# Seven half-size products instead of eight in the gated feed-forward layers of a diffusion trunk

## The chip, the cores and the metric

The kernel runs on one core of a Trainium2 chip. Its engines work side by side, each through its own queue in order: TensorE (PE in the profile) multiplies matrices into PSUM, VectorE (DVE) and ScalarE (ACT) work elementwise and read PSUM, GpSimd (POOL) works elementwise on SBUF, and SyncE (SP) issues the loads from DRAM. The metric is the device time of one execution in microseconds, lower is better.

## The reference

A trunk of two layers runs over 512 latent and 256 context tokens of 1024 channels. Each layer has a gated feed-forward half-step, a token mixer (a diagonal state space model "S5" in the first layer, gated linear attention "GLA" in the second) and a second feed-forward half-step; every one of these is preceded by an RMS norm whose scale, shift and gate come from a conditioning vector (adaLN). Cut to the part that matters here:

```python
def rmsnorm(x, w):
    return x * lax.rsqrt(jnp.mean(x * x, axis=-1, keepdims=True) + NORM_EPS) * w

def swiglu_ffn(h, w_in, w_out):                 # w_in (1024, 2 * 2816), w_out (2816, 1024)
    g, u = jnp.split(jnp.einsum('bld,df->blf', h, w_in), 2, axis=-1)
    return jnp.einsum('blf,fd->bld', jax.nn.silu(g) * u, w_out)

def ffn_half_step(x, w_norm, shift, scale, gate, w_in, w_out):
    h = rmsnorm(x, w_norm) * (1.0 + scale) + shift
    return x + 0.5 * gate * swiglu_ffn(h, w_in, w_out)

mod_x = jnp.einsum('bd,de->be', jax.nn.silu(c), ada_w[i]) + ada_b[i]    # adaLN: 9 * 1024 columns
```

All data are float32. There are four feed-forward half-steps; this document counts them one to four. Steps one, two and three are computed for all 768 tokens, step four for the latent tokens only.

## The kernel before

**Layout.** The residual stream `xT` lies in SBUF with channels on the 128 partitions: 8 channel tiles of 768 tokens. A float32 product is made of float32r parts: each operand is split into `hi` (rounded by ScalarE) and `lo` (the remainder, made by VectorE), and `mm3` (L109 to L115) adds three matmuls, hi x hi, hi x lo and lo x hi. The normed tokens are `h`, both parts, 8 channel tiles.

**Weights.** `weight` (L77) loads a unit of 128 x 1024 from DRAM into one of four buffers `wraw`, ScalarE casts it to `whi` (L88) and VectorE makes `wlo` (L89). `slot` (L92) gives the place: five pairs, or eight while the pool `more` is open, which it is during steps two and three.

**A feed-forward step** (`ffn`, L221). The hidden layer has 22 tiles of 128 columns, each with a gate and a value half. `unit(j)` (L247) loads both halves of tile j, one unit each. `hidden` (L251) multiplies the 8 channel tiles of each half by a range of tokens into two PSUM banks, then silu on ScalarE (L263), the product on VectorE (L264), and the split of the result into `mh` (L265) and `ml` (L266). Most tiles go over two ranges of 384 tokens (`parts`); the first four tiles (`lead`) go over thirds of 256 tokens (`first`), so that the norms of later tokens run while the first third is multiplied. After each group of hidden tiles (`bounds`: 4, 4, 4, 2, 4, 4) `product` (L268) multiplies them with `w_out` and adds the gated sum to `xT` on VectorE (L275). The last group goes by thirds of the tokens (`last`), and each finished third starts the norm of the next step (`after`).

**Norms.** `squares` (L142) sums squares over channel tiles on ScalarE and VectorE. The rest is put off by a counted number of steps (`later`, `tick`, L118 to L122): the sums over partitions and Newton's steps for 1/sqrt (`rstd`, L154), three steps later `spread` (L178) brings the result to all partitions, and `rest` (L196) scales each channel tile (L201) and splits it into `h` with the shift (`split`, L215: ScalarE L218, VectorE L219). `ensure` (L128) issues at once whatever is still put off that the tokens to come need.

**Fillers.** The adaLN modulation of later norms is computed beside the hidden tiles: `by_vector` (L426) loads one block of 1024 x 512 weights as four units into `wraw`, multiplies and adds them on VectorE (L435, L437: 16 operations of 512 columns), transposes and sums (L442, L443), and ends with four small matmuls. `fill` gives a list of such blocks, six in step two and nine in step three, and `filler` (L240) issues them evenly between the tiles.

**Order.** The program is written in an order of priority; a scheduler that simulates the engines' times fixes each engine's queue from it when the kernel is built. In between steps one and two stands the S5 mixer, which ends in a gated product (`glu`, L923) whose last three of eight output tiles go by thirds, as they start the norms of step two.

Of the kernel before, what the change touches and what calls it, by code (L numbers as in the profile page):

```python
# [8 lines left out]
F32 = mybir.dt.float32  # L9
F32R = mybir.dt.float32r  # L10
# [14 lines left out]
UNIT = 1024        # columns of a unit of weights  # L25


def fview(t, off, dims, p0=0, n=P):
    """A view of a tile: partitions p0..p0+n, the free dims as (step, count) pairs from element off."""
    b = t[p0:p0 + n]  # L30
    return bass.AP(b.tensor, b.offset + off, [list(b.ap[0])] + [list(d) for d in dims])


def dview(ap, off, dims):
    """A view of a DRAM tensor with dims as (step, count) pairs from element off of the AP."""
    return bass.AP(ap.tensor, ap.offset + off, [list(d) for d in dims])


class Core:
    """Shared pools, constants and the building blocks used by every phase."""  # L40

    def __init__(self, tc, stack):
# [18 lines left out]
        self.more, self.nmore = None, 0  # L61

# [29 lines left out]
    def slot(self, hi, dtype=F32R):  # L92
        """A unit's place: one of five, or of those of a further pool."""
# [6 lines left out]

    def raw(self):
# [7 lines left out]
    def mm3(self, out, w, wcols, a, first, last):  # L109
        """out += w^T a with w = (hi, lo), a = (hi, lo) pairs of f32r APs."""  # L110
# [17 lines left out]
    def ensure(self, token=TOK):  # L128
        """No work is put off any more that tokens before this one need."""
# [48 lines left out]
    def spread(self, y):  # L178
        """Columns of 128 tokens to [P, tokens] in PSUM, the same on every partition."""
# [29 lines left out]
    def norm_split(self, s, e, sc, sh, steps=0, gap=3):  # L209
        """The norm into the operand h."""  # L210
# [3 lines left out]

    def split(self, hi, lo, t, col):  # L215
        """(hi, lo) = t + col, exactly in two f32r parts."""
# [4 lines left out]
    def ffn(self, tokens, first, parts, last, gate, w_in, w_out, mids_pool, fill=lambda: (), after=None, early=0,  # L221
            spared=0, ending=None):
# [1391 lines left out]
```

## Time and profile before

| | |
|---|---|
| median of three runs | 2954.92 us (2949.38 to 2956.03) |
| span of the profiled execution | 2955.6 us |
| instructions | 45053 |
| mean granted TensorE clock | 0.971 |
| POOL instructions | 40, all short |
| loads of `w_in`, `w_out`, `ada_w` into `wraw` | 176, 88 and 97 of 512 KB |

The profiled execution's span lies inside the three runs. The page gives each engine's busy time over the span and then follows the chain of work that ended last, back from the last instruction. Busy shares are means over stages: the span cut in forty slices shows where they differ.

```profile
PE   6999999997899999999999999999999899899997
DVE  8798988635686365646435665666368777643434
PEclk9999999998899999999999999999999899899998
```

Each digit is the busy share of a slice of 74 us in tenths. Steps two and three are slices 15 to 30, where PE's row is all nines and DVE's is mostly 3 to 6; step one is slices 2 to 10, with the preparation of the S5 mixer on VectorE beside it.

### The profile page before, as it was taken

To read this page: it belongs to the slowest core of one execution; us is meant where nothing else is said; L and a number is where in the kernel's file an instruction comes from. 1 tells how busy PE (TensorE), PEld (TensorE's weight loads), DVE (VectorE), ACT (ScalarE), POOL (GpSimd) and SP (SyncE) were. 2 spreads that over 40 slices of the span, in tenths; PEclk is the share of its full clock that TensorE was granted. 3 is DMA by queue.
4 is the path that set the end of the run, shared out by engine and by line. 5 is a ranking of instruction groups with operands and counts; after the bars stand their busy time and mean duration, and the time that the engine had idled before them with its cause. 6 is when DMAs were issued, how large, how long until landed. Compare 5 with 4: busy or idle time off the path is not lost.

```text
span 2955.6 us, 45053 instructions
## 1 busy us (share of the span) xinstructions
PE 2835.5 (96%) x18303; PEld 2640.2 (89%) x18303; DVE 1813.1 (61%) x4006; ACT 891.4 (30%) x1432; POOL 8.7 (0%) x40
## 2 busy tenths in 40 slices
PE   6999999997899999999999999999999899899997
PEld 4999999997558999999999999999998788788886
DVE  8798988635686365646435665666368777643434
ACT  6321121223645242121213321111245453332221
POOL 0000000000000000000000000000000000000000
PEclk9999999998899999999999999999999899899998
DMA  7434444524776123423311342434202112233320
GB/s 227 129 101 127 106 126 125 145 90 142 229 241 181 43 65 108 121 72 107 93 58 58 93 122 86 124 98 114 56 20 86 44 51 65 65 116 98 93 79 29
DMA packets 396045, 305.45 MB, mean 103 GB/s; under 512 B 57994, under 2 KB 344188, under 8 KB 395836
## 3 DMA queue, kind: packets, MB, share of 16 engines
q1 hardware_dynamic: 382908, 289.97, 33.5%
q10 hardware_dynamic: 12928, 12.59, 1.3%
q8 instruction: 144, 2.36, 0.3%
q14 instruction: 65, 0.53, 0.1%
HBM read 275.77 MB, written 30.41 MB: 104 GB/s over the span
## 4 chain that ended last, share of the span: by engine, by line
PE 84%; DVE 9%; DMA 3%; ACT 3%; issue 2%; SPq 0%; ACTq 0%; DVEq 0%
PE bank L113 24%; PE bank L114 24%; PE bank L115 24%; PE bank L412 2%; DVE s5e L514 1%; DVE s5g L514 1%; DVE wlo L89 1%; PE bank L818 1%; PE aux L715 1%; PE aux L1244 1%; DVE s5t L514 1%; PE bank L182 1%; PE bank L1112 1%; PE bank L1113 1%; PE bank L1111 1%
## 5 line engine op out<-in xcount | busy, mean ns | idle before, releaser
L114 PE MATMUL bank<-h,whi 128*128 128x384 f32 (+3 forms) x3160 | 1052.7, 334 | 1.8 <-DVE h L939 1.8
L115 PE MATMUL bank<-h,wlo 128*128 128x384 f32 (+3 forms) x3160 | 1052.2, 334 | 0.0
L113 PE MATMUL bank<-h,whi 128*128 128x384 f32 (+3 forms) x3160 | 1048.0, 335 | 3.2 <-ACT whi L88 1.8
L88 ACT CAST whi<-wraw 128x1024 fp32r<-128x1024 f32 (+1 forms) x321 | 335.8, 1048 | 983.8 <-PE bank L114 948.3
L114 PEld LDWEIGHTS bank<-h,whi 128*128 128x128 f32 (+1 forms) x3160 | 599.2, 190 | 19.9 <-DVE h L939 2.5
L113 PEld LDWEIGHTS bank<-h,whi 128*128 128x128 f32 (+1 forms) x3160 | 596.3, 190 | 22.7 <-ACT whi L88 2.1
L115 PEld LDWEIGHTS bank<-h,wlo 128*128 128x128 f32 (+1 forms) x3160 | 597.9, 189 | 17.0 <-issue 0.2
L89 DVE TENSOR_TENSOR wlo<-wraw,whi 128x1024 fp32r<-128x1024 f32 (+1 forms) x321 | 390.7, 1219 | 282.9 <-ACT whi L88 274.0
L114 PE MATMUL bank<-ml,whi 128*128 128x384 f32 (+2 forms) x1360 | 444.6, 328 | 0.0
L115 PE MATMUL bank<-mh,wlo 128*128 128x384 f32 (+2 forms) x1360 | 444.0, 328 | 0.0
L113 PE MATMUL bank<-mh,whi 128*128 128x384 f32 (+2 forms) x1360 | 443.3, 330 | 0.2
L264 DVE TENSOR_TENSOR sg<-sg,bank 128x384 f32<-128x384 f32 (+2 forms) x166 | 89.7, 540 | 382.5 <-PE bank L115 370.6
L275 DVE SCALAR_TENSOR_TENSOR xT<-bank,hg,xT 128x256 f32<-128x256 f32 (+3 forms) x488 | 229.2, 500 | 132.3 <-PE bank L115 131.4
L113 PEld LDWEIGHTS bank<-mh,whi 128*128 128x128 f32 x1360 | 255.8, 188 | 7.8 <-ACT mh L265 0.8
L115 PEld LDWEIGHTS bank<-mh,wlo 128*128 128x128 f32 x1360 | 255.9, 188 | 6.6 <-issue 0.2
L114 PEld LDWEIGHTS bank<-ml,whi 128*128 128x128 f32 x1360 | 256.0, 188 | 6.5 <-issue 0.2
L437 DVE SCALAR_TENSOR_TENSOR adaacc<-wraw,cs,adaacc 128x512 f32<-128x512 f32 x266 | 187.6, 746 | 22.5 <-DMA wraw<-in_ada_w_dram 22.2
L265 ACT CAST mh<-sg 128x384 fp32r<-128x384 f32 (+2 forms) x166 | 83.4, 503 | 384.3 <-DVE sg L264 383.7
L263 ACT ACTIVATE sg<-bank 128x384 f32<-128x384 f32 (+2 forms) x166 | 79.4, 478 | 181.9 <-PE bank L115 181.3
L266 DVE TENSOR_TENSOR ml<-sg,mh 128x384 fp32r<-128x384 f32 (+2 forms) x166 | 89.8, 541 | 32.1 <-ACT mh L265 31.9
L150 ACT ACTIVATE sq<-xT 128x256 f32<-128x256 f32 (+1 forms) x126 | 52.9, 428 | 77.2 <-DVE xT L275 54.5
L151 DVE TENSOR_TENSOR ssq<-ssq,sq 128x256 f32<-128x256 f32 (+1 forms) x126 | 54.8, 436 | 28.6 <-ACT sq L150 26.7
(306 smaller groups left out, 2557.7 us busy)
## 6 DMA issues: line engine op xcount, KB each, us to landing
wraw<-in_ffn_w_in_dram SPq DMA_DIRECT2D x176, 512.0 KB, 4.0
wraw<-in_ada_w_dram SPq DMA_DIRECT2D x97, 512.0 KB, 3.7
wraw<-in_ffn_w_out_dram SPq DMA_DIRECT2D x88, 512.0 KB, 3.5
wraw<-in_gla_w_in_dram SPq DMA_DIRECT2D x24, 512.0 KB, 3.9
s5R<-s5r ACTq DMA_DIRECT2D x16, 512.0 KB, 3.6
s5O<-s5g SPq DMA_DIRECT2D x64, 128.0 KB, 2.4
wlo<-in_ada_w_dram SPq DMA_DIRECT2D x16, 512.0 KB, 8.1
wraw<-in_s_w_glu_dram SPq DMA_DIRECT2D x16, 512.0 KB, 4.0
```

The costliest lines, as they stand in the source:

```text
L88: nc.scalar.copy(out=hi[:, :n], in_=raw[:, :n])
L89: nc.vector.tensor_tensor(out=lo[:, :n], in0=raw[:, :n], in1=hi[:, :n].bitcast(F32), op=ALU.subtract)
L113: mm(out, wh, a[0], start=first, stop=False)
L114: mm(out, wh, a[1], start=False, stop=False)
L115: mm(out, wl, a[0], start=False, stop=last)
L263: nc.scalar.activation(sg, banks[0][:, :e - s], AF.Silu)
L264: nc.vector.tensor_mul(sg, sg, banks[1][:, :e - s])
L265: nc.scalar.copy(out=mh[:, o], in_=sg)
L266: nc.vector.tensor_tensor(out=ml[:, o], in0=sg, in1=mh[:, o].bitcast(F32), op=ALU.subtract)
L275: nc.vector.scalar_tensor_tensor(out=self.xT[:, d, a:z], in0=b[:, a - s:z - s], scalar=gate[i][:, d:d + 1], in1=self.xT[:, d, a:z], op0=AL ...
L437: nc.vector.scalar_tensor_tensor(out=acc[:, v], in0=w[:, k], scalar=col, in1=acc[:, v], op0=ALU.mult, op1=ALU.add)
L514: self.c.nc.vector.tensor_tensor(out=out, in0=a, in1=b, op=op)
```

## The change

In steps two and three the first product of a hidden tile is done by Strassen's method in Winograd's form. The 8 channel tiles are cut in an upper and a lower half, the tokens in blocks of 128 that are even or odd, and a tile's columns in gate and value. That makes a product of 2 x 2 blocks by 2 x 2 blocks, which takes seven block products in place of eight, each over 4 channel tiles and half of the tokens.

- `unit` loads the same two units as before. GpSimd makes four sums of half-units in place, and `half` splits each of seven half-units of 512 columns into its two parts, two half-units to a slot.
- `norm_seven` replaces the split of the norm: beside the four blocks of `h` it makes four further sums on VectorE, three of which go with both parts into a new tile `hx`; it uses four `wraw` buffers for each 256 tokens.
- `hidden_seven` runs the seven products, each into a bank of its own (84 matmuls over half of the tokens), and VectorE combines them: seven sums that each read a bank, two products, two remainders.
- One leading tile in place of four, over the token ranges (0, 512) and (512, 768); the other 21 tiles go over all tokens at once.
- adaLN blocks are given to the filler in quarters (one load and four VectorE operations each, the finish with the last).
- The pool `more` isn't open in these steps (the slots are five pairs); in `glu` the last two tiles go by thirds, not three.

The core of the diff (comments that fall away, and the renaming of arguments, are left out):

```diff
+    def half(self, raw):
+        nc = self.nc
+        if self.pending is None:
+            self.pending = w = self.slot(True), self.slot(False)
+            hi, lo = (t[:, :HALF] for t in w)
+        else:
+            hi, lo = (t[:, HALF:] for t in self.pending)
+            self.pending = None
+        nc.scalar.copy(out=hi, in_=raw)
+        nc.vector.tensor_tensor(out=lo, in0=raw, in1=hi.bitcast(F32), op=ALU.subtract)
+        return hi, lo
...
+    def norm_seven(self, s, e, sc, sh, steps=0, gap=3):
...
+        def rest(y):
+            r = self.spread(y)
+            for g in range(2):
+                v, w = (self.raw().rearrange("p (a i t) -> p a i t", i=2, t=t) for t in (2 * P, P))
+                for i in range(2):
+                    for lower in range(2):
+                        k, t = 4 * lower + 2 * g + i, v[:, lower, i]
+                        nc.vector.scalar_tensor_tensor(out=t, in0=self.xT[:, k, s:e], scalar=sc[:, k:k + 1], in1=r,
+                                                       op0=ALU.mult, op1=ALU.mult)
+                        nc.scalar.activation(t, t, AF.Identity, bias=sh[:, k:k + 1])
...
+                for x, minuend, less, (hi, lo) in ((b11, None, None, place(0, 0)), (t1, b12, b11, place(0, 1)),
+                                                   (t2, b22, t1, beside(0)), (b21, None, None, place(1, 0)),
+                                                   (t3, b22, b12, beside(1)), (b22, None, None, place(1, 1)),
+                                                   (t4, b21, t2, beside(2))):
+                    if less is not None:
+                        nc.vector.tensor_tensor(out=x, in0=minuend, in1=less, op=ALU.subtract)
+                    nc.scalar.copy(out=hi, in_=x)
+                    nc.vector.tensor_tensor(out=lo, in0=x, in1=hi.bitcast(F32), op=ALU.subtract)
...
-        lead = 4 if self.more else 2
-        bounds = [0, 4, 8, 12, 14, 18, FT] if self.more else [0, 2, 6, 10, 14, 18, FT]
+        lead = 1 if seven else 4 if self.more else 2
+        bounds = [0, 4, 8, 12, 14, 18, FT] if self.more or seven else [0, 2, 6, 10, 14, 18, FT]
...
+            def both(out, i0, i1, op):
+                nc.gpsimd.tensor_tensor(out=out, in0=i0, in1=i1, op=op)
+                return self.half(out)
+            return [self.half(a11), both(a21, a21, a22, ALU.add), both(a11, a21, a11, ALU.subtract), self.half(a12),
+                    both(a21, a22, a11, ALU.subtract), both(a12, a12, a11, ALU.subtract), self.half(a22)]
+
+        def hidden_seven(j, w, s, e):
...
+            nc.scalar.copy(out=g1, in_=part(0, 0))
+            p5 = part(1, 1)
+            plus(g2, g1, part(2, 4))
+            plus(g1, g1, part(3, 2))
+            nc.scalar.activation(g1, g1, AF.Silu)
+            plus(u1, g2, part(4, 5))
+            plus(g2, g2, p5)
+            plus(u2, u1, p5)
+            plus(g2, g2, part(5, 3))
+            nc.scalar.activation(g2, g2, AF.Silu)
+            nc.vector.tensor_mul(u2, u2, g2)
+            mid(u2, 1)
+            plus(u1, u1, part(6, 6))
+            nc.vector.tensor_mul(u1, u1, g1)
+            mid(u1, 0)
...
-            if j < KT - 3:
+            if j < KT - 2:
...
+        return [lambda p=p: unit(p) for p in range(3)] + [lambda: (unit(3), finish())]
...
-                ffn(0, 1, both, thirds, halves, thirds, mp,
-                    lambda: rest(6, mp) + [lambda: (mods.scale(1, 0), mods.half_gate(1, 0))], norm(1, 0))
+                ffn(0, 1, both, pieces, halves, thirds, mp,
+                    lambda: rest(6, mp) + [lambda: (mods.scale(1, 0), mods.half_gate(1, 0))], norm_seven(1, 0),
+                    seven=True)
```

More of the change, by code (lines that the diff above doesn't have):

```diff
@@ L25 @@
 UNIT = 1024
+HALF = UNIT // 2
 def fview(t, off, dims, p0=0, n=P):
@@ L248, in unit @@
             mids[j] = [mids_pool.tile([P, n], F32R, tag=t, name=t, bufs=nfc) for t in ("mh", "ml")]
-            return [self.weight(win[:, :, q * F + j * P:q * F + (j + 1) * P]) for q in range(2)]
+            if not seven:
+                return [self.weight(win[:, :, q * F + j * P:q * F + (j + 1) * P]) for q in range(2)]
+            raw = [self.raw() for q in range(2)]
+            for q in range(2):
+                self.dma(raw[q].rearrange("p (k f) -> p k f", k=KT), win[:, :, q * F + j * P:q * F + (j + 1) * P])
@@ L283, in ffn @@
             for j in range(lead):
-                hidden(j, ws[j], s, e, j == 0)
+                if seven:
+                    hidden_seven(j, ws[j], s, e)
+                else:
+                    hidden(j, ws[j], s, e, j == 0)
         todo = list(fill())
@@ L291, in ffn @@
                 w = unit(j)
-                for s, e in parts:
-                    hidden(j, w, s, e, False)
+                if seven:
+                    hidden_seven(j, w, *tokens)
+                else:
+                    for s, e in parts:
+                        hidden(j, w, s, e, False)
                 filler()
@@ L438, in by_vector, with finish @@
                                                        op0=ALU.mult, op1=ALU.add)
[L439 to L450 removed]
+        def finish():
+            sums = pool.tile([P, 32], F32, tag="adas", name="adas", bufs=1)
+            for v in range(2):
+                turned = self.c.tmp.tile([P, 512], F32, tag="sg", name="adat", bufs=2)
+                nc.vector.transpose(turned, acc[:, v])
+                nc.vector.tensor_reduce(out=sums[:, 16 * v:16 * v + 16], in_=turned.rearrange("p (b x) -> p b x", x=32),
+                                        axis=mybir.AxisListType.X, op=ALU.add)
+            t = self.c.aux()
+            for g in range(4):
+                nc.tensor.matmul(t[32 * g:32 * g + 32, :8], self.quarter, fview(sums, g, [(4, 4), (16, 2)]),
+                                 start=True, stop=True)
+            self.columns(l, m, q, t)
+        return [lambda p=p: unit(p) for p in range(3)] + [lambda: (unit(3), finish())]
     def columns(self, l, m, q, t):
```

95 lines of the change are left out of this document (69 added, 26 removed).

## The prediction

> **What bounds the kernel now.** I read the profile's page first: engine totals, then the chain of work that ended last.
>
> ```profile
> PE 2835.5 (96%) x18303; PEld 2640.2 (89%) x18303; DVE 1813.1 (61%) x4006; ACT 891.4 (30%) x1432; POOL 8.7 (0%) x40
> PE 84%; DVE 9%; DMA 3%; ACT 3%; issue 2%; SPq 0%; ACTq 0%; DVEq 0%
> ```
>
> TensorE (PE) is on the path for 84% of the span, and POOL does nearly nothing. A mean says little of one stage, so I cut the span into windows. Feed-forward step two runs from about 1046 to 1605 us and step three to about 2173 (the bursts of xT updates by L275 show the ends).
>
> ```profile
> 1046.00:1605.00 559.00, 559.00 (x3502) 557.11 (x3501) 290.22 (x518) 130.00 (x208) 0.00 (x0) 1.00 0.29 85
> 1605.00:2173.00 568.00, 565.11 (x3556) 562.42 (x3555) 329.81 (x604) 130.09 (x209) 0.37 (x3) 1.00 0.32 94
> 1750.00:1800.00 50.00, 50.00 (x292) 49.73 (x292) 31.95 (x53) 10.01 (x14) 0.00 (x0) 1.00 0.39 112
> 1050.00:1100.00 50.00, 50.00 (x424) 50.00 (x423) 25.34 (x68) 18.82 (x41) 0.00 (x0) 1.00 0.01 3
> ```
>
> The columns after each window's length are the busy time and count of PE, weight loads, DVE (VectorE), ACT (ScalarE) and POOL, then the granted clock, DMA share and GB/s. PE never rests in step two and only 3 us in step three, at a clock of 1.00; DVE is busy 52% and 58%. **Both steps are bound by the number of matmuls.** The last two rows give the price: 50/292 = 0.171 us for a matmul with 384 columns, 50/424 = 0.118 us with 256.
>
> **What TensorE saves.** A hidden tile now takes 96 matmuls of 384 columns (2 halves, 2 products, 8 channel tiles, 3 terms): 16.4 us. After, 7 products x 4 x 3 = 84 of 384: 14.4 us, 2.05 less. Four tiles of each step go by thirds now, 144 x 0.118 = 17.0 us each; three of them come to 14.4, the first to 84 of 256 and 84 of 128 columns. No 128-column matmul of this kind is in the trace. Following the line from 384 to 256 gives 0.065 us; the bounds are that and 0.118, which would add 4.5 us a step. I take 0.065, so the first tile costs 15.4. Per step: 18 x 2.05 + 3 x 2.6 + 1.6 = 46.3; two steps **-93 us**. The gated product ahead of them moves one tile from thirds to halves: 17.0 - 16.4, -0.5. The last products of the steps stay.
>
> **What VectorE gets.** Durations in both steps, by shape:
>
> ```profile
> L89 DVE TENSOR_TENSOR wlo<-wraw,whi 128x1024 fp32r<-128x1024 f32 x128 | 156.4, 1222 | 116.4 <-ACT whi L88 115.6
> L437 DVE SCALAR_TENSOR_TENSOR adaacc<-wraw,cs,adaacc 128x512 f32<-128x512 f32 x210 | 147.8, 745 | 16.0 <-DMA wraw<-in_ada_w_dram 15.6
> L266 DVE TENSOR_TENSOR ml<-sg,mh 128x384 fp32r<-128x384 f32 x72 | 39.6, 551 | 16.2 <-ACT mh L265 16.2
> L264 DVE TENSOR_TENSOR sg<-sg,bank 128x384 f32<-128x384 f32 x72 | 39.5, 549 | 217.8 <-PE bank L115 215.3 <-PE aux L448 2.5
> L442 DVE STREAM_TRANSPOSE adat<-adaacc 128x512 f32<-128x512 f32 x30 | 21.1, 703 | 0.1
> L443 DVE TENSOR_REDUCE adas<-adat 128x16 f32<-128x512 f32 x30 | 20.3, 676 | 0.2
> L514 DVE TENSOR_TENSOR s5t<-s5asc,s5ct x32: 669/681/768, 186.1 to 558.8; 128x512 f32<-128x512 f32 x32
> ...
> 2140.69 0.55 DVE L266 TENSOR_TENSOR ml<-sg,mh 128x384 fp32r<-128x384 f32 x1
> 2141.16 0.48 DVE L275 SCALAR_TENSOR_TENSOR xT<-bank,hg,xT 128x256 f32<-128x256 f32 x1
> ```
>
> The last two rows, from the timeline, show that in a full queue the next instruction starts 0.08 us before the end of the one in front: a 384-column operation occupies 0.47 us, not 0.55. I subtract 0.08 throughout. A tile now takes 2 weight splits of 1024 columns and 4 operations of 384: 2 x 1.14 + 4 x 0.47 = 4.2 us. After, it takes 7 splits of 512 (0.681, so 0.60) and 11 operations of 384 (seven sums that each read a PSUM bank, two products and two remainders): 7 x 0.60 + 11 x 0.47 = 9.4 us. That is +5.2 a tile, +114 a step. Against the windows: 290 + 114 + 16 (norms, below) = 420 of 513 us in step two, 330 + 130 = 460 of 519 in step three. Can PE stay full beside that?
>
> ```profile
> 150.00:200.00 50.00, 50.00 (x316) 49.68 (x316) 45.26 (x139) 13.75 (x22) 0.52 (x1) 1.00 0.37 110
> ```
>
> Yes: in step one DVE is 91% busy in this window and PE does not rest. But it is closer inside the tiles. A quarter block of adaLN is 4 x 0.70 plus a quarter of the finish (two transposes, two sums, 0.7): 3.5 us. 24 quarters over 26 filler steps make 3.2 us a tile in step two, 36 make 4.85 in step three. So DVE has 12.6 us of work beside 14.4 of PE in step two, and **14.25 beside 14.4 in step three**; there nothing is left to hide a wait in.
>
> **What POOL gets.** Four sums of 128x512 a tile. The trace has no such operation; the nearest rows:
>
> ```profile
> L514 DVE TENSOR_TENSOR s5g<-s5asc,s5ct x32: 1097/1133/1220, 196.1 to 554.9; 128x512 f32<-128x512 f32 x32
> L670 POOL MEMSET s5cb<- 128x512 f32 x8 | 4.2, 525 | 504.1 <-PE aux L715 484.2 <-PE bank L1441 19.9
> masks.py:199 POOL TENSOR_SCALAR_AFFINE_SELECT ident<-ident 128x128 f32<-128x128 f32 x1 | 0.3, 292 | 0.0
> masks.py:197 POOL MEMSET ident<- 128x128 f32 x1 | 0.2, 204 | 0.3 <-POOLq L1603 0.3
> 336.05 4.12 DVE L514 TENSOR_TENSOR s5g<-s5asc,s5ct 128x512 f32<-128x512 f32 x4 [0.87 <-PE aux L715]
> ```
>
> The memsets give 0.10 us plus 0.84 ns a column, the one that reads a tile 1.5 ns a column; with a second input 2.2, so 1.23 us for 512 columns, an estimate. The bounds are 0.525 (only writing) and 1.66 (twice the one that reads). Four are 4.9 us of 14.4, so POOL itself is no bound; a half is ready about 2.5 us after its sum starts (sum, ACT's copy, DVE's split), and the five weight slots hold ten halves of which a tile uses seven, so that chain is hidden while DVE is not late.
>
> What a POOL sum costs DVE is the open price. Bounds: 0, and 1.23 us for each, if DVE stands still for its whole length. The only overlap in the trace is a memset (0.53 us at 336.13) beside the first of four DVE operations of the last row, 4.12/4 = 1.03 each, no longer than the group's median in the first row (1133 ns). It shows no loss, but a memset reads nothing. I take 0.3 us a sum, nearer to that row: 1.2 a tile. Step two then has 13.8 beside 14.4, hidden. Step three has 15.45, so 1.05 x 21 tiles = **+22 us**.
>
> **The two starts.** Norms change too: for 256 tokens DVE now does 16 large operations, after it 30 (8 scalings, 8 sums of operands, 14 remainders). The start of step three on the timeline and in windows:
>
> ```profile
> 1600.00:1610.00 10.00, 7.11 (x59) 6.86 (x59) 9.21 (x25) 5.49 (x11) 0.00 (x0) 1.00 0.63 188
> 1040.00:1050.00 10.00, 10.00 (x88) 10.00 (x88) 9.64 (x22) 6.15 (x12) 0.00 (x0) 1.00 0.65 210
> ...
> 1605.41 0.48 DVE L275 SCALAR_TENSOR_TENSOR xT<-bank,hg,xT 128x256 f32<-128x256 f32 x1
> ...
> 1608.31 0.43 DVE L151 TENSOR_TENSOR ssq<-ssq,sq 128x256 f32<-128x256 f32 x1
> 1608.66 0.47 DVE L201 SCALAR_TENSOR_TENSOR nt<-xT,sc,bank 128x256 f32<-128x256 f32 x1
> 1609.05 0.15 DVE L174 TENSOR_TENSOR rs<-rs 128x2 f32<-128x2 f32 x1
> ```
>
> The last product ends at 1605.3; the first third's norm starts at 1608.66 and PE rests 2.9 us, because its first piece needs that third alone. After, the first piece is tokens 0 to 512: both thirds must be normed. At 0.39 us a scaling and 0.35 a sum (next starts above), 30 are 11 us; the second third's operands are there after some two thirds of its 30. 1608.66 + 11 + 7.5 = 1627: PE waits 22 us, 19 more. The next piece (84 x 0.118 = 9.9 us) ends at 1637; the last third's operands come after the 4 us that are left of the second, 4 us of the first tile's own sums and 7.5: 1642, 5 more. That is +24, and as much at the start of step two, where today PE does not rest (second window): **+48**. Bounds: 0, if the norms go ahead of the last product's end, and +35 each, if the tile's weights come late as well (the norms now borrow four of the same four raw buffers that its loads need). DVE was full from 1600 to 1610 already, so I stay above the middle.
>
> ```profile
> L88 ACT CAST whi<-wraw 128x1024 fp32r<-128x1024 f32 x128 | 134.5, 1051 | 477.2 <-PE bank L114 477.2
> L265 ACT CAST mh<-sg 128x384 fp32r<-128x384 f32 x72 | 36.8, 511 | 172.5 <-DVE sg L264 172.4
> ```
>
> ACT goes from 2 casts of 1024 columns and 4 operations of 384 (4.1 us a tile) to 7 of 512, 0.62 on the line between these rows, and 5 of 384: 6.9 us, far under 14.4. SP issues the same loads; an adaLN block's four come one by one. PSUM has six banks, and one product stays for three others, so PE can run some five products, 10 us, ahead of DVE; a wait that is longer stops it. Behind a DVE instruction that waits for POOL stand the evacuations, and PE waits for those.
>
> **Sum:** -93 - 0.5 + 22 + 48 = -23. The span is 2955.6, inside the three runs (2949.4 to 2956.0, median 2954.9), so what lies around it is under half a microsecond. **Forecast 2933 us**, 0.8% faster.
>
> **Rivals.** *Nothing new waits* (norms hidden, POOL free): -93, 2862. For it speaks the window at 91%; against it the full queue at 1600.
>
> *POOL's sums hold VectorE up* (slower). If every DVE operation that reads two SBUF tiles stands still while a sum runs, the wait is the share of such work: in step three 7 x 0.60 + 4 x 0.47 + 3.4 of adaLN = 9.5 of 14.25, 67%, so 0.82 us a sum and 3.3 a tile. Step two: 12.6 + 3.3 = 15.9, +1.5; step three 17.55, +3.15; x 21 = +98. Sum -94 + 48 + 98 = +52, 3008. It decides from 0.52 us a sum on, where 21 x (8 x 0.52 - 1.95) = 46 eats what the starts leave. For it speaks that all of a tile's slack is gone in step three; the trace has no such overlap. The Trainium skill, "SBUF — State Buffer", section "Who interferes with whom", states just this: VectorE with two SBUF inputs and a GpSimd instruction that reads SBUF exclude each other for the whole instruction; no run here shows it yet, and by that rule the time is this rival's.
>
> *It doesn't do what it says:* not possible for the count of matmuls, which is in the code.
>
> **Chances.** Forecast's case (2905 to 2948) 0.36; nothing waits, wholly or mostly (under 2905) 0.24; between, within 0.2% 0.10; POOL's rival (above 2961) 0.30. 0.2%, 6 us, is about what a measurement can tell here. Faster 0.60, same 0.10, slower 0.30. Range 2865 to 3010: below it lies full success, above it waits of the whole sum (1.23 us each give 3075), together under 0.2.
>
> **What would show it.** Some 740 matmuls fewer in the two steps, at 0.171 us. DVE's splits of 512 at 0.68 us and its 384-column operations at 0.55: if they measure over 0.9 beside POOL, the rival holds. The windows of tiles in step three: PE under 95% means DVE is the bound. PE's idle at both starts: some 22 and 5 us. Wrong would be all of it if POOL's sums took over 3 us each, as then weights come late.

## The result, and the profile after

The changed kernel takes **2970.97 us** in the median of four runs (2967.23 to 2977.41), the kernel before 2954.15 beside it: a ratio of 1.0064, with a 95% interval of 1.0048 to 1.0080. It is slower, by some 17 us where 22 faster were forecast. Its profiled execution has a span of 2965.5 us at a mean clock of 0.960 (before 2955.6 at 0.971).

The same two lines of the page as before, engine totals and chain, and PE's row of slices:

```profile
PE 2779.8 (94%) x17511; PEld 2572.5 (87%) x17511; DVE 2154.4 (73%) x4623; ACT 1022.3 (34%) x1773; POOL 283.3 (10%) x216
PE   6999999997899989999997899999999899799997
...
PE 62%; DVE 22%; DMA 6%; issue 6%; ACT 3%; POOL 0%; SPq 0%; DVEq 0%; ACTq 0%; POOLq 0%
```

792 matmuls are gone and PE's busy time is 56 us less (2835.5 before), and still the end comes later: the path runs over PE for 62% of the span instead of 84%, over DVE for 22% instead of 9%. The dents in PE's row, an 8 in slice 15 and a 7 and an 8 in slices 22 and 23 where the kernel before has 9s, are the starts of steps two and three.

I cut both traces by the same three marks: the start of the last sigmoid of the gated product ahead of step two, and the end of the last `xT` update of each step. The timeline rows of the changed kernel for these (start, duration):

```profile
1029.53 0.48 ACT L1090 ACTIVATE sg<-bank,cols 128x256 f32<-128x256 f32 x1 [0.28 <-PE bank L130]
...
1596.17 1.06 DVE L397 SCALAR_TENSOR_TENSOR xT<-bank,hg,xT 128x256 f32<-128x256 f32 x2
...
2178.05 0.48 DVE L397 SCALAR_TENSOR_TENSOR xT<-bank,hg,xT 128x256 f32<-128x256 f32 x1
```

| us | before | changed | difference |
|---|---|---|---|
| to the last sigmoid | 1044.8 | 1029.5 | -15.3 |
| step two | 561.1 | 567.7 | +6.6 |
| step three | 567.8 | 581.3 | +13.5 |
| behind it, to the end of the span | 781.9 | 787.0 | +5.1 |

So the two steps, which lose an eighth of their first products, become **20 us longer**. Inside them, the windows of the changed kernel (length; PE, weight loads, DVE, ACT, POOL busy; clock):

```profile
1029.50:1080.00 50.50, 34.77 (x194) 32.48 (x194) 47.66 (x145) 33.20 (x85) 7.73 (x5) 0.67 0.15 43
1080.00:1560.00 480.00, 468.61 (x2663) 463.91 (x2663) 392.44 (x641) 150.58 (x266) 128.98 (x80) 0.99 0.32 95
1597.00:1670.00 73.00, 49.31 (x307) 47.74 (x307) 65.03 (x172) 37.87 (x97) 13.67 (x10) 0.79 0.25 73
1670.00:2140.00 470.00, 452.18 (x2558) 444.17 (x2557) 407.91 (x668) 142.34 (x250) 114.27 (x75) 0.98 0.34 103
```

At the two starts (rows one and three) PE rests 15.7 and 23.7 us and works at a clock of 0.67 and 0.79. In the tiles (rows two and four) it rests 11.4 and 17.8 us, where the kernel before rested in neither (480.00 of 480 and 470.00 of 470 us busy in the same windows). DVE is 94% and 89% busy at the starts and 82% and 87% in the tiles. The waits of PE over both steps (sum, times, longest):

```profile
PE bank L197 <- DVE rs L190: 17.1, 2, 10.4
PE bank L128 <- ACT mh L350: 12.8, 8, 2.5
PE bank L128 <- DVE ssq L354: 10.2, 5, 7.0
PE bank L128 <- ACT h L274: 7.9, 4, 4.3
PE bank L129 <- DVE ml L351: 5.8, 6, 1.7
PE bank L128 <- DVE nt L354: 5.4, 3, 3.5
```

`rs` and `h` belong to the norms of the starts. `mh`, `ml`, `ssq` and `nt` are the evacuation and the split of hidden tiles. The 7.0 us for `ssq`, at 1646, still belong to the start of step three, where its second tile begins; the others lie in the tiles, so VectorE is late there too. The groups by shape from 1020 to 2210 us say why:

```profile
L324 POOL TENSOR_TENSOR wraw<-wraw 128x512 f32<-128x512 f32 x173 | 270.2, 1563 | 855.2 <-DVE wlo L113 371.6 <-DMA wraw<-in_ffn_w_in_dram 176.6 <-issue 83.7
L113 DVE TENSOR_TENSOR wlo<-wraw,whi 128x512 fp32r<-128x512 f32 x306 | 227.5, 765 | 30.9 <-ACT whi L112 29.6
L572 DVE SCALAR_TENSOR_TENSOR adaacc<-wraw,cs,adaacc 128x512 f32<-128x512 f32 x210 | 184.8, 902 | 41.6 <-DMA wraw<-in_ada_w_dram 41.6
L351 DVE TENSOR_TENSOR ml<-nt,mh 128x384 fp32r<-128x384 f32 x84 | 59.2, 715 | 1.4
L370 DVE TENSOR_TENSOR nt<-nt,sg 128x384 f32<-128x384 f32 x42 | 36.6, 871 | 0.3
L367 DVE TENSOR_TENSOR nt<-nt,ssq 128x384 f32<-128x384 f32 x42 | 28.3, 673 | 1.9 <-ACT ssq L366 1.8
L354 DVE TENSOR_TENSOR ssq<-ssq,bank 128x384 f32<-128x384 f32 x84 | 45.9, 546 | 1.2 <-PE bank L130 0.5
```

A GpSimd sum takes 1.56 us, not 1.23. And VectorE's operations with two inputs in SBUF are longer than the prediction's free durations: the split 765 ns (681), adaLN's product 902 (745), the remainder `ml` 715 (551). The last row reads a PSUM bank and keeps its 546. One such stop can be seen in the timeline:

```profile
1642.98 1.38 POOL L324 TENSOR_TENSOR wraw<-wraw 128x512 f32<-128x512 f32 x1 [1.36 <-DVE wlo L113]
1643.16 1.75 DVE L572 SCALAR_TENSOR_TENSOR adaacc<-wraw,cs,adaacc 128x512 f32<-128x512 f32 x1
...
1645.43 0.74 DVE L572 SCALAR_TENSOR_TENSOR adaacc<-wraw,cs,adaacc 128x512 f32<-128x512 f32 x1
```

The sum runs from 1642.98 to 1644.36. The adaLN product that starts 0.18 us after it takes 1.75 us, just over 1.00 more than the same product at 1645.43 with no sum beside it.

### The profile page after: what moved, and what is told of

Same layout as the page of the kernel before. It is cut to its first block, busy times and chain, and to the rows that moved or that the text cites. A ratio compares the mean times of both kernels' runs of the same rounds, so it can differ in the third digit from the quotient of the medians.

```text
span 2965.5 us, 44922 instructions
## 1 busy us (share of the span) xinstructions
PE 2779.8 (94%) x17511; PEld 2572.5 (87%) x17511; DVE 2154.4 (73%) x4623; ACT 1022.3 (34%) x1773; POOL 283.3 (10%) x216
## 4 chain that ended last, share of the span: by engine, by line
PE 62%; DVE 22%; DMA 6%; issue 6%; ACT 3%; POOL 0%; SPq 0%; DVEq 0%; ACTq 0%; POOLq 0%
PE bank L129 17%; PE bank L130 17%; PE bank L128 17%; DVE adaacc L572 4%; DMA wraw<-in_ada_w_dram 3%; DVE wlo L113 3%; DVE wlo L91 2%; PE bank L541 2%; DVE s5g L652 1%; DVE s5e L652 1%; DVE ml L351 1%; DVE ssq L354 1%; PE aux L853 1%; DVE nt L370 1%; DMA wraw<-in_ffn_w_in_dram 1%
## 5 line engine op out<-in xcount | busy, mean ns | idle before, releaser
L128 PE MATMUL bank<-h,whi 128*128 128x384 f32 (+2 forms) x2344 | 795.0, 343 | 19.9 <-DVE ssq L354 8.8
L129 PE MATMUL bank<-h,whi 128*128 128x384 f32 (+2 forms) x2344 | 799.3, 342 | 2.5 <-DVE h L275 2.2
L130 PE MATMUL bank<-h,wlo 128*128 128x384 f32 (+2 forms) x2344 | 797.5, 341 | 0.0
L128 PEld LDWEIGHTS bank<-h,whi 128*128 128x128 f32 x2344 | 444.8, 191 | 42.5 <-ACT h L274 9.4
L129 PEld LDWEIGHTS bank<-h,whi 128*128 128x128 f32 x2344 | 446.1, 190 | 21.5 <-DVE h L275 3.1
L130 PEld LDWEIGHTS bank<-h,wlo 128*128 128x128 f32 x2344 | 446.0, 190 | 16.9
L90 ACT CAST whi<-wraw 128x1024 fp32r<-128x1024 f32 x233 | 243.8, 1048 | 522.8 <-PE bank L129 472.4
L91 DVE TENSOR_TENSOR wlo<-wraw,whi 128x1024 fp32r<-128x1024 f32 x233 | 283.6, 1220 | 162.9 <-ACT whi L90 154.5
L324 POOL TENSOR_TENSOR wraw<-wraw 128x512 f32<-128x512 f32 x176 | 274.6, 1562 | 967.4 <-DVE wlo L113 384.5
L113 DVE TENSOR_TENSOR wlo<-wraw,whi 128x512 fp32r<-128x512 f32 x308 | 228.8, 764 | 33.4 <-ACT whi L112 32.1
L128 PE MATMUL bank<-hx,whi 128*128 128x384 f32 (+2 forms) x552 | 186.1, 337 | 1.8 <-ACT hx L274 1.5
L129 PE MATMUL bank<-hx,whi 128*128 128x384 f32 (+2 forms) x552 | 185.8, 337 | 0.2 <-DVE hx L275 0.2
L130 PE MATMUL bank<-hx,wlo 128*128 128x384 f32 (+2 forms) x552 | 185.5, 336 | 0.0
```

What stands on the lines that cost most here:

```text
L90: nc.scalar.copy(out=hi[:, :n], in_=raw[:, :n])
L91: nc.vector.tensor_tensor(out=lo[:, :n], in0=raw[:, :n], in1=hi[:, :n].bitcast(F32), op=ALU.subtract)
L113: nc.vector.tensor_tensor(out=lo, in0=raw, in1=hi.bitcast(F32), op=ALU.subtract)
L128: mm(out, wh, a[0], start=first, stop=False)
L129: mm(out, wh, a[1], start=False, stop=False)
L130: mm(out, wl, a[0], start=False, stop=last)
```

## The experiments

The runs of the kernel before beside each set of experiments have medians of 2949 to 2951 us, and of 2954 beside the changed kernel, so I compare ratios to it, and differences between kernels of two sets are differences of their ratios times 2950 us. The changed kernel stands at 1.0064. Two theories come first. **A:** a GpSimd sum stops those VectorE operations that read two SBUF tiles. **B:** the starts are the price, since VectorE has 30 large operations for each third instead of 16.

**Quarters alone** (`e1_quarters`). The kernel before with adaLN by quarters, nothing else of the change.

```diff
-            return [vec(*blocks.pop(0), pool) for _ in range(n)]
+            return [f for _ in range(n) for f in vec(*blocks.pop(0), pool)]
```

> The kernel before with one part of the change alone: adaLN on VectorE by quarters of blocks, its transposes in another pool (the seven products are not made). In the two profiles the gated product before step two begins 12 us earlier after the change, and until there nothing else of it is at work. If the quarters are the cause, this kernel is 8 to 14 us faster than before, about 2943, and the seven products and what goes with them cost 28 us of their own. If that was the scheduler's drift from other lines, it is within 4 us of before.

Measured 2949.01 us, ratio 0.9997 (0.9988 to 1.0006): no effect that can be told. The division of adaLN neither gives nor costs.

**No sums** (`e2_no_sums`). The changed kernel with unsummed halves as the weights of the seven products, so that GpSimd has nothing to do in the steps.

```diff
-            return [self.half(a11), both(a21, a21, a22, ALU.add), ...
+            return [self.half(t) for t in (a11, a21, a11, a12, a21, a12, a22)]
```

> The changed kernel with GpSimd's four sums of each tile left out, so that the seven products multiply unsummed half-units. Theory A, GpSimd's sums stop VectorE operations that read two SBUF tiles: splits of 512 columns go from 0.766 back to 0.68 us, adaLN's operations from 0.90 to 0.745, ml from 0.715 to 0.55, and the time falls by 35 to 60 us, to about 2925. Theory B, the norms at the two starts are what costs: VectorE's durations may fall, but the time falls by under 12 us.

Measured 2926.09, ratio 0.9916 (0.9901 to 0.9931). The sums cost 1.5% of the time, some 44 us: theory A's range, where B had under 12. Its groups, with L571 and L350 for the lines 572 and 351 above:

```profile
L113 DVE TENSOR_TENSOR wlo<-wraw,whi 128x512 fp32r<-128x512 f32 x306 | 201.6, 684 | 23.6 <-ACT whi L112 23.4
L571 DVE SCALAR_TENSOR_TENSOR adaacc<-wraw,cs,adaacc 128x512 f32<-128x512 f32 x210 | 151.6, 745 | 31.7 <-DMA wraw<-in_ada_w_dram 31.5
L350 DVE TENSOR_TENSOR ml<-nt,mh 128x384 fp32r<-128x384 f32 x84 | 44.8, 549 | 1.4
```

All three are back at their free durations. The growth beside the sums can now be added up from the busy times of the five groups: 227.5 - 201.6 for the splits, 184.8 - 151.6 for adaLN, 59.2 - 44.8 for `ml`, and 13.5 and 5.2 for the two products (23.1 each here): 92 us over 176 sums, **0.52 us a sum**.

**Sums on VectorE** (`e3_sums_vector`). The same four sums, complete, by the other engine.

```diff
-                nc.gpsimd.tensor_tensor(out=out, in0=i0, in1=i1, op=op)
+                nc.vector.tensor_tensor(out=out, in0=i0, in1=i1, op=op)
```

> The changed kernel with the four sums of each tile on VectorE in place of GpSimd. They add 176 x 0.60 = 106 us of VectorE work in steps two and three and take away the waits for GpSimd. Theory A: the waits are 91 us of VectorE's time (the sum of what its durations grew by), so the time is within 15 us of the changed kernel's 2971. If the waits cost little, VectorE has 106 us more to do where it is full already: 3010 or more.

Measured 2936.55, ratio 0.9955 (0.9941 to 0.9968): some 32 us faster than the changed kernel, and faster than the kernel before. Both expectations missed it: A had it within 15 us of the changed kernel, its rival at 3010 or more.

```profile
L324 DVE TENSOR_TENSOR wraw<-wraw 128x512 f32<-128x512 f32 x173 | 117.5, 683 | 24.4 <-DMA wraw<-in_ffn_w_in_dram 24.2
L113 DVE TENSOR_TENSOR wlo<-wraw,whi 128x512 fp32r<-128x512 f32 x306 | 202.7, 682 | 15.0 <-ACT whi L112 14.9
```

A sum takes VectorE 0.68 us, little more than the 0.52 us by which the same sum on GpSimd stops it. VectorE's busy time in the whole execution is the same (2158.0 us, changed kernel 2154.4): giving the work away freed nothing.

**Stop or late chain?** In the changed kernel a half also comes late, as it passes from GpSimd through ScalarE to VectorE, whose later work queues behind the split. Theory **C** gives that the price. Two kernels separate them. In one (`e5_sums_unread`) the sums run but nobody reads them:

```diff
+            w = [self.half(a11), self.half(a11)]
+            for i0, i1 in ((a21, a22), (a21, a12), (a22, a12), (a12, a21)):
+                nc.gpsimd.tensor_tensor(out=a11, in0=i0, in1=i1, op=ALU.add)
+            return w + [self.half(t) for t in (a21, a12, a21, a12, a22)]
```

> The weights go in as without sums (work left out: the seven products use unsummed halves), but GpSimd computes its four sums a tile all the same, into a half that is already split; nobody reads them. Theory A (a GpSimd sum stops VectorE's operations on two SBUF tiles while it runs): the splits of 512 columns measure 740 ns or more and adaLN's 850 or more, as in the changed kernel, and the time is 2955 to 2975 us. Theory C (what costs is the chain DMA, GpSimd, ScalarE, VectorE, in which a half is late and VectorE's later work queues behind its split): no chain is here, so 2922 to 2935 us, whatever single operations measure.

In the other (`e6_memsets`) the chain stays and GpSimd reads nothing:

```diff
-                nc.gpsimd.tensor_tensor(out=out, in0=i0, in1=i1, op=op)
+                for _ in range(3):
+                    nc.gpsimd.memset(out, 0.5)
```

> The chain without reads: at the place of each GpSimd sum stand three GpSimd memsets of the same 512 columns (3 x 0.53 = 1.6 us, as long as a sum measured), so the halves are as late and the same waits remain (work left out: the sums). Theory A (GpSimd's reads stop VectorE): VectorE's operations are back at 682, 745 and 549 ns, and the time is 2922 to 2940 us. Theory C (the late halves cost): 2955 to 2975 us with VectorE's operations at their free durations.

Measured 2994.58, ratio 1.0156 (1.0139 to 1.0173), for the unread sums, and 2927.09, ratio 0.9918 (0.9901 to 0.9936), for the memsets. The groups, unread sums first:

```profile
L328 POOL TENSOR_TENSOR wraw<-wraw 128x512 f32<-128x512 f32 x172 | 280.3, 1629 | 872.1 <-DVE wlo L113 703.8 <-DMA wraw<-in_ffn_w_in_dram 66.3 <-DVE ssq L356 65.5
L113 DVE TENSOR_TENSOR wlo<-wraw,whi 128x512 fp32r<-128x512 f32 x305 | 237.9, 805 | 24.6 <-ACT whi L112 24.5
```

```profile
L325 POOL MEMSET wraw<- 128x512 f32 x519 | 270.0, 529 | 807.8 <-DVE wlo L113 479.3 <-DMA wraw<-in_ffn_w_in_dram 215.2 <-DVE ssq L355 50.2
L113 DVE TENSOR_TENSOR wlo<-wraw,whi 128x512 fp32r<-128x512 f32 x306 | 204.2, 684 | 30.6 <-ACT whi L112 30.3
L573 DVE SCALAR_TENSOR_TENSOR adaacc<-wraw,cs,adaacc 128x512 f32<-128x512 f32 x210 | 152.1, 745 | 28.1 <-DMA wraw<-in_ada_w_dram 28.0
```

GpSimd is busy for 280 and 270 us in the two. Where it reads, the splits take 805 ns, and the time goes up although nothing waits for its results; where it only writes, they take 684 and the time is that of no sums at all, although everything waits for it. Theory C falls, and theory A holds for what stops VectorE; its time for the unread sums was missed. They cost some 27 us more than the changed kernel's own, outside the range (2955 to 2975). They also hold the weights' buffers for longer, and whether that is the cause wasn't tried.

**Slack for VectorE.** 5 of the 16 adaLN products of a block remain in steps two and three, with GpSimd's sums (`e7_light_pool`) and without any (`e8_light_none`).

```diff
-                for k in range(2):
+                for k in range(1 if light else 2):
+                    if light and part and v:
+                        continue
```

> The changed kernel with most of adaLN's products left out in steps two and three (5 of 16 operations a quarter block remain), so that VectorE has 2 us and more of slack in a tile; GpSimd's sums stay. Theory A with the capacity of the prediction (lost time counts only where VectorE has no slack): within 12 us of the same kernel without the sums, where the full adaLN shows 45. Theory C (late halves, or a stop that hits whatever is urgent): 30 us or more slower than the same kernel without the sums.

> As the run before, without GpSimd's sums (work left out: the sums and most of adaLN's products). What is left over the saved matmuls is the starts of the two steps. If these alone are the rest, 2905 to 2925 us: the tiles then run at TensorE's pace (before - 85 + some 45 to 55 for two starts). If the tiles still wait for VectorE without both, over 2925.

Measured 2935.98, ratio 0.9949 (0.9931 to 0.9966), and 2915.67, ratio 0.9881 (0.9867 to 0.9896). The difference is 20 us where the full adaLN shows 44: between the two expectations. The kernel without sums is inside its own range (2905 to 2925). The windows of the tiles in step two and step three, with sums and without:

```profile
1080.00:1560.00 480.00, 479.99 (x2787) 477.75 (x2787) 355.05 (x603) 157.27 (x282) 125.08 (x84) 0.99 0.32 95
1690.00:2120.00 430.00, 423.44 (x2453) 419.35 (x2452) 319.57 (x540) 132.42 (x235) 101.38 (x72) 0.99 0.34 102
```

```profile
1080.00:1560.00 480.00, 480.00 (x2814) 478.11 (x2813) 323.60 (x602) 156.72 (x280) 0.00 (x0) 1.00 0.32 95
1690.00:2120.00 430.00, 429.89 (x2571) 426.88 (x2570) 299.74 (x568) 138.27 (x249) 0.37 (x3) 1.00 0.34 102
```

With slack the sums cost nothing in the tiles of step two: PE is busy 479.99 of 480 us, and from 1200 to 1440 us it runs 1385 matmuls with sums and 1386 without. In the 430 us of step three, where adaLN is denser, it rests 6.6 us. Without sums the tiles run at TensorE's pace, and the steps take 545.7 and 547.7 us. With them they take 550.3 and 563.3. In step two those 4.6 us are lost around the start: from 1060 to 1080 us the clock is 0.70 there, against 0.93 without sums.

**The starts.** These kernels stand on the one with the sums on VectorE (2936.55) unless it is said otherwise. Norms that begin after fewer products (`e9_norms_early`):

```diff
-            s5.glu(yp, halves, thirds, norm_seven(0, 2, 12))
+            s5.glu(yp, halves, thirds, norm_seven(0, 2, 6))
...
-                    ... norm_seven(1, 0),
+                    ... norm_seven(1, 0, 4),
```

> Sums on VectorE (as in e3_sums_vector, 2936.6 us), and the norms ahead of steps two and three begin after 6 and 4 products instead of 12 and 9, so that a third's norm runs beside the last products of the step before. Theory B (the price of a start is VectorE's 30 operations a third behind the last product): the first two thirds are ready some 5 to 10 us earlier at each start, 2915 to 2930 us. Rival (what is late at a start is the last third's sums, or the half clock that follows any rest): 2932 to 2942 us.

Measured 2948.10, ratio 1.0001 (0.9991 to 1.0012): some 14 us slower, a miss for both. PE waits 15.8 us for `ssq` there (4.3 with the late norms): the 30 operations of an early third stand in VectorE's queue ahead of the sums of squares of the next.

The plain norm, with the sums of operands a constant (`e10_plain_norms`):

```diff
-                for x, minuend, less, (hi, lo) in ((b11, None, None, place(0, 0)), ...
+                self.split(self.h[:, 0, k, s:e], self.h[:, 1, k, s:e], t, sh[:, k:k + 1])
```

> As e3_sums_vector, but the norms of steps two and three write the plain operand only, with 16 large operations a third as before the change; the three sums of operands are a constant (work left out) and the weights' buffers aren't borrowed. Theory B (the 14 added operations are the price of the starts): 2885 to 2905 us, some 20 us a start less. Rival (the first piece of 512 tokens, which waits for two norms, and the half clock are the price): 2915 to 2930 us.

Measured 2915.34, ratio 0.9892 (0.9876 to 0.9907): some 20 us less, on the edge of the rival's range. By time, the 14 added operations a third, with the borrowed buffers, cost some 10 us a start, not the 20 that theory B gives. By the marks the two steps are 27 us shorter (542.8 + 546.9 against 557.0 + 559.8), but the last sigmoid ahead of them comes 5 us later, so 10 to 14 us a start is as near as this comes.

And the first tile's division. By thirds, on the changed kernel (`e4_thirds_first`):

```diff
-            pieces = [(0, 512), (512, 768)]
+            pieces = thirds
```

> The changed kernel with the first tile of a step over three thirds of the tokens, not over (0, 512) and (512, 768). Theory B1, TensorE waits at the starts because its first piece needs two normed thirds: it starts some 10 us earlier and the time falls by 10 to 20 us, to about 2955. Theory B2, the start is as long as VectorE's norms of all three thirds, with only one tile of products to cover them: the second tile begins no earlier, and the time is within 5 us of 2971.

Measured 2999.09, ratio 1.0167 (1.0153 to 1.0181): some 30 us slower than the changed kernel and a miss for both theories, although PE begins 5 us behind the last sigmoid, at 1038.67, and not 15 us behind it as in the changed kernel. Its windows inside the first tile, and behind it:

```profile
1042.00:1058.00 16.00, 16.00 (x77) 16.00 (x76) 8.42 (x33) 5.08 (x13) 0.00 (x0) 0.50 0.00 0
1066.00:1100.00 34.00, 34.00 (x162) 34.00 (x161) 26.57 (x70) 16.86 (x46) 7.27 (x5) 0.50 0.34 93
1104.00:1120.00 16.00, 16.00 (x94) 16.00 (x93) 13.21 (x19) 5.78 (x11) 6.42 (x5) 1.00 0.29 88
```

34 us at half clock with PE busy throughout: 162 matmuls of 128 columns at 0.210 us. In one piece: with early norms (`e11_whole_first`), with the norms where the change has them (`e12_whole_sums_vector`), and on the changed kernel with GpSimd's sums (`e13_whole_sums_pool`):

```diff
-            pieces = [(0, 512), (512, 768)]
+            pieces = [both]
```

> As e9_norms_early, with the first hidden tile in one piece of 768 tokens instead of 512 and 256. A matmul of 128 columns took as long as one of 256 in the changed kernel (0.114 us at full clock, 0.213 at half), so one piece needs 84 x 0.171 = 14.4 us of TensorE where two need 84 x (0.118 + 0.114) = 19.5. If the last third's norm is hidden behind the early ones, 5 us a start less than e9_norms_early; if the first tile then waits for it, 5 to 15 us more in all.

> The sums on VectorE and the norms where the change has them (e3_sums_vector, 2936.6 us), with the first hidden tile in one piece of 768 tokens. Theory D (the second piece costs 5 us of TensorE at each start, since its 128-column matmuls take as long as 256-column ones, and the short rests before it bring a second stretch at half clock, some 13 us that cost 6 more): 2915 to 2928 us. Rival (one piece waits longer for the last third's norm and gives it back): 2932 to 2942 us.

> The changed kernel (2971 us) with one edit, the first hidden tile in one piece; the sums stay on GpSimd. Theory D: the starts gain the same 10 to 22 us here as with the sums on VectorE, 2949 to 2961 us, and what is left over e12_whole_sums_vector is GpSimd's price in the tiles, 30 to 40 us. Rival (starts and sums are one queue on VectorE, and a start's gain is lost in the tiles): 2963 us or more.

Measured 2934.34 (ratio 0.9953, 0.9940 to 0.9965), **2929.71 (0.9935, 0.9921 to 0.9948)** and 2961.25 (1.0043, 1.0030 to 1.0056). Against the same kernels with two pieces, one piece gains 14, 6 and 6 us by the ratios (14, 7 and 10 by the medians). With the norms where the change has them, both results lie between theory D's range and its rival's, and their intervals overlap those of the kernels with two pieces (0.9941 to 0.9968, 1.0048 to 1.0080). So the division is worth some 3 us a start there, hardly clear of noise, and 7 with early norms. Why one piece isn't worth more can be seen in a window of the second kernel at the start of step three:

```profile
1590.00:1615.00 25.00, 7.68 (x23) 6.48 (x24) 24.04 (x81) 15.99 (x45) 0.00 (x0) 0.50 0.00 0
```

PE rests 17.3 of these 25 us, since one piece waits for all three norms, and DVE is full (24.0): what is left of the start is VectorE's. The same sums on GpSimd cost 31.5 us here, in a kernel with another start. The second of these is the fastest kernel of the study with all of the computation: 0.65% faster than the kernel before.

## Why the prediction was wrong

The steps of its sum, with what the runs show. The lengths of both steps are the traces' own, by the marks above (before 561.1 and 567.8, together 1128.9). Each is one execution, and the quarters' kernel, whose steps are those of the kernel before but for the quarters, shows 1125.6: a term is good to some 3 us.

| term | forecast | shown | from |
|---|---|---|---|
| matmuls of the two steps | -93 | -84 | 128-column price, below |
| the two starts | +48 | +49 | 545.7 + 547.7 without sums and with light adaLN, less 1128.9 - 84 |
| VectorE's load, without POOL | 0 | +13 | 550.2 + 555.8 without sums, less the former |
| POOL's sums | +22 | +43 | 567.7 + 581.3, less the latter |
| both steps | -23 | +20 | |

**POOL's sums: the step that failed.** The prediction bounded the price for VectorE between 0 and 1.23 us a sum and took 0.3, since a memset beside a VectorE operation in the trace showed no loss; it said itself that a memset reads nothing. The runs give 0.52, which happens to be the point from which it let the rival decide; the rival's own 0.82, a stop for the whole of a sum, was too high. The nearest row was of the wrong kind: memsets in place of the sums, 519 of them, lengthen none of the groups shown, while sums that nobody reads do. The page that it named for the rival (the Trainium skill, "SBUF — State Buffer", section "Who interferes with whom") makes just this difference: VectorE with two SBUF inputs contends with a GpSimd instruction that reads SBUF, not with one that only writes. The traces agree on each side: 765 ns against 681, 684 beside memsets, 546 unchanged with a PSUM input. With a mechanism known, the row to weigh was the one that shares it.

With 0.52 in place of 0.3, the prediction's own rule gives (12.6 + 2.08 - 14.4) x 21 = 6 us in step two and (14.25 + 2.08 - 14.4) x 21 = 41 in step three, 46 in all beside the 43 that were measured. That nearness is in part luck, since the rule's load was too high: by the prediction's own rows, with 0.08 taken off, a quarter block of adaLN is 4 x 0.665 + 0.61 = 3.3 us and not 3.5, and the rule then gives 2 + 34 = 36 us. (The six banks on which it lets PE run ahead are the kernel's pool `bank`, with `bufs=6`.) The term was too small by 21 us of the 43 between -23 and +20; of the other 22, 8 are the 128-column matmuls, 13 VectorE's load and 1 the starts.

**"Hidden" in step two: only roughly.** The 43 are divided otherwise than the rule says: step two lost 17.5 us to the sums (550.2 to 567.7), step three 25.5. The light kernels show that slack does hide the stops, some 2 us a tile of them entirely in step two. With a few tenths to spare the mean of a tile says too little, for work isn't even. PE's waits for `mh` and `ml` stand at the ends of the groups of tiles, where no other product is ready: at 1135, 1233, 1328 and 1476 us in step two, each 1.6 to 2.5 us and each just ahead of a burst of `xT` updates.

**VectorE's load: the right count, the wrong cover.** Without any sum the two steps still lose 13 us against light adaLN. The window of step one with VectorE 91% busy and PE full was taken for proof that such a load is hidden. There it was other work in another order. The windows of the tiles of the kernel without sums and with full adaLN:

```profile
1080.00:1560.00 480.00, 477.28 (x2773) 474.68 (x2773) 360.63 (x661) 154.45 (x277) 0.00 (x0) 1.00 0.32 95
1690.00:2120.00 430.00, 426.96 (x2517) 423.15 (x2516) 345.69 (x637) 135.56 (x243) 0.37 (x3) 1.00 0.34 104
```

PE rests 2.7 and 3.0 us in them, so less than half of the 13 is rest in these windows; the remainder lies outside them, around the starts and the ends of the steps.

**The starts: right as a sum, partly by luck.** 49 us against 48. The prediction's arithmetic gives some 10 of a start's 24 to the first piece of two thirds and some 14 to the added operations: with 16 operations a third, the second third would be ready at 1608.66 + 5.9 + 4 = 1618.6 and not 1627, and the last third would hold up nothing. The plain norm bears that out with 10 to 14 us. But the rests were sized too high, and a half clock was missing. The starts of the light kernel without sums:

```profile
1032.40:1080.00 47.60, 29.76 (x198) 28.15 (x198) 45.70 (x146) 33.14 (x86) 0.00 (x0) 0.75 0.18 48
1578.10:1640.00 61.90, 43.31 (x275) 41.87 (x274) 54.69 (x163) 37.09 (x96) 0.00 (x0) 0.81 0.31 87
```

PE rests 17.8 and 18.6 us, 36 in all, where the forecast amounts to some 24 and 27, with the 2.9 of today. While it works it is granted 0.75 and 0.81 of its clock, which costs some 11 us more, an estimate (busy time times the part of the clock that is missing, in windows of 5 us). Two errors of opposite sign made the sum come out.

**What TensorE saves: a bound came true.** A matmul of 128 columns was taken at 0.065 us, on the line through 384 and 256, with 0.118 as the bound. The timeline of the changed kernel in the first tile's second piece:

```profile
1060.26 0.29 PE L130 MATMUL bank<-hx,wlo 128*128 128x256 f32 x1
1060.39 0.28 PE L128 MATMUL bank<-hx,whi 128*128 128x256 f32 x1
...
1061.03 0.28 PE L130 MATMUL bank<-h,wlo 128*128 128x128 f32 x1
1061.14 0.27 PE L128 MATMUL bank<-h,whi 128*128 128x128 f32 x1
...
1065.18 0.41 PE L128 MATMUL bank<-hx,whi 128*128 128x128 f32 x1
1065.40 0.41 PE L129 MATMUL bank<-hx,whi 128*128 128x128 f32 x1
```

A start every 0.11 to 0.13 us with 256 columns, every 0.11 with 128, and every 0.21 at half clock: below 256 columns a matmul isn't cheaper here. 2 x 84 x (0.114 - 0.065) = 8 us, the step from -93 to -84.

**Around the steps.** The gated product gave 3.4 us by the profile, for 0.5. The 12 us that the profile is shorter ahead of it aren't explained; the quarters alone, without effect on the time, show 5 of them. The 5 us more behind the steps are within the scatter: over all kernels here that part takes 781 to 788 us.

Right were the count of matmuls (744 fewer in the steps and 48 in the gated product, the 792 that are gone), that POOL itself is no bound (283 us busy), and where to look: the prediction would have given its rival the case with splits over 0.9 us; at 0.765 in the mean the time came out between the two, 2971 beside 2933 and 3008. Its other sign, PE under 95% in the tiles of step three, was set too far off as well: 96% there went with a loss.

What stays open: why 92 us of stops cost some 43 us while 117 us of sums in VectorE's own queue cost 11 (557.0 + 559.8 in the two steps, less 550.2 + 555.8). That the order of the queues, which is fixed when the kernel is built, knows of the sums but not of the stops is an argument, not shown.

## What to carry to other kernels

Before work is given to GpSimd to relieve VectorE, look at what VectorE runs beside it: if that reads two SBUF tiles, the sum comes back as a stop (0.52 us each here) and doing it on VectorE (0.68 us) can be the faster way. Price an unknown by the row that shares the mechanism, not by the one with the nearest name; if no row does, let the range's end that hurts decide whether the plan stands. A saving at TensorE's pace counts only as far as the engine that feeds it has slack in every tile, and here, at the seams between phases, the norm set the time and not the product.

## What the runs showed of the hardware

**Half clock holds through 128-column matmuls.** In the kernel with thirds first, the clock stays at 0.50 from 1042 to 1100 us although PE is busy for 54 of these 58 us, and is back at 1.00 once matmuls of 384 columns run (the third row of its windows above). The changed kernel does the same in its second piece, from 1065 to 1078 us; its first matmul of 384 columns starts at 1077.98, and at 1081 their durations fall from 0.52 to 0.34 us:

```profile
1066.00:1077.00 11.00, 11.00 (x54) 11.00 (x53) 8.76 (x15) 5.49 (x12) 6.35 (x5) 0.50 0.51 144
```

Yet at full clock such a stretch can pass without a drop: in the kernel with plain norms, in whose second piece PE rests for 0.4 us in 9,

```profile
1065.00:1074.00 9.00, 8.64 (x78) 8.50 (x77) 8.89 (x23) 5.45 (x14) 0.00 (x0) 1.00 0.04 7
```

the 128-column matmuls run at 1.00. So once the clock is lost (after a rest of 1.15 us that ends at 1062.79 in the changed kernel) 128-column matmuls didn't bring it back in these runs, and wider ones did. Nor does every rest lose it, as an expectation above has it. What exactly loses it wasn't tried by itself. The Trainium skill, "TensorE: Matmul & The Clock Gate", section "Part 1: The HAM clock gate", has the clock back after some 3.4 us of sustained work; here 34 us at 128 columns didn't do it, and the measurement decides.

**GpSimd's sums spread too.** A sum of 128x512 in the changed kernel takes from 1.26 to 3.62 us, 1.56 in the mean, and 1.63 in the mean where nobody reads the sums and they come in a row. That VectorE holds GpSimd up is the likely cause, but no run has the sums without VectorE beside them. And one group of VectorE with a single SBUF tile to read is longer too: adaLN's first product, 479 ns without sums, 552 in the changed kernel, 555 beside memsets, 814 beside the unread sums, while the transposes of the same width stay at 702 to 704.
